# Mixer of a two-layer block: per-head rows in DRAM, loads four heads ahead, softmax rows scaled on GpSimd

## The chip, the cores and the metric

The kernel runs on one NeuronCore of a Trainium2 chip. The metric is device time in microseconds of one launch: 3129.61 us is the median of three runs (3122.44 to 3131.08) of the kernel before. The traces are of one profiled execution each. Engines are named as in the profile: PE (TensorE matmul), PEld (its weight load), DVE (VectorE), ACT (ScalarE), POOL (GpSimd), SP (SyncE, which issues nearly all DMAs here).

## The reference, cut to what matters

A first block (gated delta rule plus banded attention, up to about 730 us of the trace) is untouched. Its output enters a second block of two layers. Each layer is a feed-forward half, the mixer, a second feed-forward half and a per-layer embedding step. Only the mixer changes; x is [512, 1024], all in float32.

```python
def hybrid_mixer(h, ...):
    z = h @ w_in
    q_lat, kv_lat, k_rope, qkv_d = jnp.split(z, [c0, c1, c2], axis=-1)
    q = (rmsnorm(q_lat, q_norm) @ w_q_up).reshape(B, S, MLA_HEADS, MLA_NOPE + MLA_ROPE)   # 8 x (64 + 32)
    q_rope = apply_rope(q[..., MLA_NOPE:], cos_m, sin_m)
    kv = (rmsnorm(kv_lat, kv_norm) @ w_kv_up).reshape(B, S, MLA_HEADS, MLA_NOPE + MLA_V)
    k_rope = apply_rope(k_rope[:, :, None, :], cos_m, sin_m)[:, :, 0]                     # one, shared by 8 heads
    o_mla = mla_attention(q_nope, q_rope, k_nope, k_rope, v_mla)        # causal softmax, 512 x 512
    qd, kd, vd = [t.reshape(B, S, DIL_HEADS, DIL_HEAD_DIM) for t in jnp.split(qkv_d, 3, axis=-1)]   # 8 x 64
    o_dil = dilated_attention(apply_rope(qd), apply_rope(kd), vd)       # three strides, merged
    merged = jnp.concatenate([rmsnorm(o_mla, ...), rmsnorm(o_dil, ...)], axis=-1)
    return merged @ w_out
```

Each of the 16 heads is softmax(q k + mask) v over 512 tokens; "m" heads are the 8 latent heads (96 rows of q and k), "d" heads the 8 dilated ones (64 rows).

## The kernel before

Activations are feature-major tiles [128, 8, 512]. A float32 operand is kept as a high part and a low part (names ending in H and L), and a product is three matmul passes over them. A scheduler lays down the order of each engine ahead of the run, so the order on an engine is not the order of the code; a DMA on SP waits its turn in SP's row, and at most eight are under way.

The mixer (L1184 to L1425 of the function that the diff touches) goes through these stages, shown with the times of layer 0:

- The projections (1100 to 1197 us): q and k of the dilated heads come from the generator `dil`, called `fill`, in steps of 24 matmuls (psn<-xn). Four steps (g = 0, heads d0 to d3) run here; four steps (g = 1, heads d4 to d7) are filler for later. Every result is split into H and L in a tile `so` of three buffers and stored to DRAM by `out()` (L1207; the store is L1210).
- The latent stage (1197 to 1240 us): 60 matmuls on latH and latL make q and k of the latent heads and their v; `out()` stores QR, QN, KN; L1182 stores VM from a tile `vo` of two buffers. KR is the shared rope part of k.
- The attention loop (1240 to 1410 us). `scores(n)` loads q and k of head n into `qh` and `kh` (two buffers each) and v into `vh`: an m head takes five loads for q and k (L1336 to L1340), a d head eight loads of 32 rows (L1348, L1349). `head_scores` then does for four blocks of 128 queries, 128, 256, 384 and 512 keys wide: matmuls psg<-kh,qh on PE (psg has three buffers), mask and row maximum on DVE (L1145, to tile S, maximum in mn), exponential on ACT (L1147), and the reciprocal of the row sums on DVE (L1149, rd). `head_values` transposes S on PE (L1162, psx<-ident,S, ten matmuls), splits it into ptH and ptL (ACT, DVE), and multiplies by v (L1172, twelve matmuls); ACT copies the result to om or od (L1397).
- `normed` (L1357 to L1365) divides by the row sums after that: for each pair of heads eight matmuls (L1363, ident times rd spread over 64 columns) put 1/sum into psn, and DVE multiplies om or od by it (L1365).
- The heads go d0 to d3, m0 to m7, d4 to d7. The loop body of head n takes a step of filler (`fill`, `late`, and `first`, which is half of the output product) and calls `scores(n + 2)`.
- The tail (1405 to 1425 us): root-mean-square norms (`group`, L1309), the output product with weights wo, and the residual onto h, the [128, 8, 512] float32 tile (2 MB) of the residual stream, which sits in SBUF through the whole mixer.

Before the diff, a d head is loaded so:

```python
for y in range(2):
    for z in range(2):
        o = 64 * z + 32 * y
        nc.sync.dma_start(qf[o:o + 32, 0], QD[g, y, r, z])
        nc.sync.dma_start(kf[o:o + 32], KD[g, y, r])
```

## Time and profile before

| what | us |
|---|---|
| median of three runs | 3129.61 |
| the profiled execution, its own time | 3144.24 |
| its span, first to last instruction | 3142.3 |
| mixer of layer 0, of layer 1 | 1100 to 1425, 2310 to 2640 |
| attention stretch of layer 0, of layer 1 | 1240 to 1410, 2450 to 2617 |

The rows further down come from five views. The page gives busy time by engine and the chain of work that ended last. The list of waits says what ended an engine's idle time. The timeline lists instructions with their start and duration; a bracket gives the idle time before an instruction and what released it. The windows give busy time by engine for a stretch, with the granted TensorE clock (1.00 is 2.4 GHz, 0.50 is 1.2 GHz) and the traffic. The groups by line give count, busy time and mean duration.

### The profile page before, as it was taken

The page shows a single profiled execution, that of the slowest core. Times are in us where ns is not written, and L with a number is a line of the kernel's source. Part 1 is how long each engine was busy: PE and PEld are TensorE (multiplying, and loading weights), DVE is VectorE, ACT ScalarE, POOL GpSimd, SP SyncE. Part 2 cuts the span into 40 slices and gives each one's busy share as a digit, 9 for nine tenths or more (in the row PEclk, how much of TensorE's full clock was granted, in tenths as well). Part 3 has the DMA queues.
Part 4 walks back from the last instruction along what each step waited for, and adds up shares of the span by engine and source line. Part 5 has one row for each costly group of instructions (what it writes and reads, how often), then busy time and mean ns, then how long its engine had stood idle before and what let it go on. Part 6 is the DMA issues. An engine that isn't in the chain of part 4 may idle for free.

```text
span 3142.3 us, 41998 instructions
## 1 busy us (share of the span) xinstructions
PE 2853.6 (91%) x16048; PEld 2392.3 (76%) x16048; DVE 1747.3 (56%) x3733; ACT 1085.4 (35%) x2062; POOL 344.7 (11%) x199
## 2 busy tenths in 40 slices
PE   7999699999999997887999988999989787999987
PEld 2877588678888885667888878888887566888877
DVE  6678907666333475468523378423376457723357
ACT  3443225443222233563322234322233464322223
POOL 3023211422000011002000022000011001000010
PEclk8999769999999998998999998999999898999998
DMA  5325341443222136542222221322234643222321
GB/s 198 98 94 173 91 125 46 146 141 102 100 88 99 59 116 219 149 137 91 94 94 97 91 94 54 111 95 97 88 83 166 178 144 118 95 94 88 100 74 54
DMA packets 151584, 344.29 MB, mean 110 GB/s; under 512 B 37616, under 2 KB 58480, under 8 KB 150872
## 3 DMA queue, kind: packets, MB, share of 16 engines
q1 hardware_dynamic: 142168, 318.55, 31.9%
q10 hardware_dynamic: 9216, 23.07, 2.1%
q8 instruction: 126, 2.06, 0.3%
q14 instruction: 74, 0.61, 0.1%
HBM read 292.02 MB, written 49.54 MB: 109 GB/s over the span
## 4 chain that ended last, share of the span: by engine, by line
PE 71%; DVE 15%; ACT 4%; DMA 4%; issue 3%; POOL 2%; SPq 0%; ACTq 0%; DVEq 0%; POOLq 0%
PE psg L87 31%; PE psx L87 27%; PE psn L87 2%; PE psx L1172 2%; DVE ss L160 2%; DVE big L512 1%; ACT wH L78 1%; DMA wraw<-in_wo 1%; PE psn L141 1%; DVE wL L80 1%; ACT S L1147 1%; DMA wraw<-in_wvd 1%; DVE h L191 1%; DVE cy L386 1%; DVE xnL L105 1%
## 5 line engine op out<-in xcount | busy, mean ns | idle before, releaser
L78 ACT ACTIVATE wH<-wraw 128x1024 fp32r<-128x1024 f32 (+2 forms) x445 | 445.1, 1002 | 1149.7 <-PE psg L87 564.8
L80 DVE TENSOR_TENSOR wL<-wraw,wH 128x1024 fp32r<-128x1024 f32 (+3 forms) x353 | 406.4, 1153 | 458.9 <-ACT wH L78 458.2
L87 PE MATMUL psg<-xnH,wH 128*128 128x512 f32 (+3 forms) x1528 | 549.2, 361 | 11.8 <-ACT xnH L101 6.4
L87 PE MATMUL psg<-xnL,wH 128*128 128x512 f32 (+3 forms) x1528 | 548.9, 360 | 8.8 <-DVE xnL L105 8.8
L87 PE MATMUL psg<-xnH,wL 128*128 128x512 f32 (+3 forms) x1528 | 549.3, 360 | 4.4 <-POOL wL L80 4.4
L80 POOL TENSOR_TENSOR wL<-wraw,wH 128x1024 fp32r<-128x1024 f32 x92 | 224.9, 2451 | 2139.6 <-ACT wH L78 927.2
L87 PE MATMUL psx<-xnH,wL 128*128 128x512 f32 (+1 forms) x1120 | 391.2, 349 | 1.6 <-POOL wL L80 1.6
L87 PE MATMUL psx<-xnH,wH 128*128 128x512 f32 (+1 forms) x1120 | 392.1, 350 | 0.1
L87 PE MATMUL psx<-xnL,wH 128*128 128x512 f32 (+1 forms) x1120 | 392.0, 350 | 0.0
L87 PEld LDWEIGHTS psg<-xnH,wH 128*128 128x128 f32 (+2 forms) x1528 | 297.3, 195 | 52.8 <-ACT xnH L101 8.0
L87 PEld LDWEIGHTS psg<-xnL,wH 128*128 128x128 f32 (+2 forms) x1528 | 297.7, 195 | 49.9 <-DVE xnL L105 11.4
L87 PEld LDWEIGHTS psg<-xnH,wL 128*128 128x128 f32 (+2 forms) x1528 | 297.9, 195 | 45.3 <-POOL wL L80 5.3
L87 PEld LDWEIGHTS psx<-xnH,wL 128*128 128x128 f32 x1120 | 217.1, 194 | 28.4 <-POOL wL L80 1.9
L87 PEld LDWEIGHTS psx<-xnH,wH 128*128 128x128 f32 x1120 | 217.7, 194 | 26.9 <-ACT wH L78 0.3
L87 PEld LDWEIGHTS psx<-xnL,wH 128*128 128x128 f32 x1120 | 217.2, 194 | 25.8
L1056 DVE TENSOR_TENSOR fa<-fs,psx 128x512 f32<-128x512 f32 (+1 forms) x104 | 62.9, 605 | 270.0 <-PE psx L87 268.9
L87 PE MATMUL psg<-aH,wH 128*128 128x512 f32 (+1 forms) x464 | 159.2, 343 | 0.0
L87 PE MATMUL psx<-aL,wH 128*128 128x512 f32 (+1 forms) x464 | 158.8, 342 | 0.0
L87 PE MATMUL psg<-aL,wH 128*128 128x512 f32 (+1 forms) x464 | 158.5, 342 | 0.0
L87 PE MATMUL psx<-aH,wL 128*128 128x512 f32 (+1 forms) x464 | 158.4, 341 | 0.0
L87 PE MATMUL psx<-aH,wH 128*128 128x512 f32 (+1 forms) x464 | 158.4, 341 | 0.0
L87 PE MATMUL psg<-aH,wL 128*128 128x512 f32 (+1 forms) x464 | 158.3, 341 | 0.0
(568 smaller groups left out, 4756.1 us busy)
## 6 DMA issues: line engine op xcount, KB each, us to landing
wraw<-in_gu SPq DMA_DIRECT2D x176, 512.0 KB
wraw<-in_dn SPq DMA_DIRECT2D x64, 448.0 KB
wraw<-in_dn SPq DMA_DIRECT2D x32, 512.0 KB
wraw<-in_wmod SPq DMA_DIRECT2D x24, 512.0 KB
wraw<-in_wrest ACTq DMA_DIRECT2D x24, 512.0 KB
wraw<-in_wo SPq DMA_DIRECT2D x24, 512.0 KB
wraw<-in_win SPq DMA_DIRECT2D x22, 512.0 KB
kh<-KD SPq DMA_DIRECT2D x64, 128.0 KB
```

What stands on the lines that cost most here:

```text
L78: nc.scalar.activation(H[:, :n], raw[:, :n], AF.Copy)
L80: e.tensor_tensor(L[:, :n], raw[:, :n], H[:, :n].bitcast(F32), op=ALU.subtract)
L87: self.nc.tensor.matmul(ps, lhsT=l, rhs=r, start=start and i == 0, stop=stop and i == m - 1)
L105: e.tensor_tensor(L, src, H.bitcast(F32), op=ALU.subtract)
L141: self.nc.tensor.matmul(ps[:, 128 * c:128 * c + 128], lhsT=rs[:, c:c + 1].to_broadcast([128, 128]), rhs=self.ident, start=True, stop=True)
L160: nc.vector.tensor_tensor(self.a[i], self.a[i], q, op=ALU.add)
L191: nc.vector.tensor_tensor(hk, hk, t, op=ALU.add)
L386: nc.vector.scalar_tensor_tensor(y, cb[:, o + j:o + j + n], cw[:, j:j + 1], y, op0=ALU.mult, op1=ALU.add)
L512: nc.vector.tensor_tensor(tm, A[:112, i:i + 1, i + 1:].to_broadcast([112, n, n]), A[:112, i + 1:, i + 1:].rearrange("q j c -> q c j"), op= ...
L1056: nc.vector.tensor_tensor(a, s, pu[:, :n], op=ALU.mult)
L1147: nc.scalar.activation(S, S, AF.Exp, bias=mn[:, i:i + 1], scale=-1.0, accum_out=den[:, i:i + 1])
L1172: nc.tensor.matmul(pv[:, 128 * j:], lhsT=V[:, j, v:v + 64], rhs=R[b][:, o0:o0 + n], start=z == 0 and y == 0, stop=z == 3 and y == 2)
```

## The change

- DRAM layout: each head has its rows together, QM and KM [8, 96, 2, 512] for m heads, QD and KD [8, 64, 2, 512] for d heads. `out()` takes a list of destinations and makes two or four smaller stores of one tile where it made one. The shared rope part of k is stored into all eight heads by two stores of 32 x 8 x 512.
- `load()`: an m head takes two loads of 96 rows, a d head four of 64 rows. qh and kh have four buffers each, in a pool that takes the room of h. Four heads are loaded right after the fourth step of `fill`, ahead of the stores of the latent stage in the code, and then one head per loop step, for n + 6.
- h is stored to DRAM (hd) after the last read of it, and loaded again after the loop. For that its pool is opened after that of xn.
- The rows of S are multiplied by 1/sum on POOL, four instructions per head (L1153 of the changed kernel); `normed` is gone, with its matmuls and its DVE multiplication.
- The loop begins at n = -2 and calls scores(n + 2) first in its body; the step of filler comes after it, and the norm of the m half (`group(om, 0)`) stands at n = 12 where it stood at 13; `first` advances two steps from n = 13 where it advanced four from 14.

The core of the diff:

```diff
-            def out(src, dst, n=128):
+            def out(src, dsts, n=128):
                 t = pr.tile([128, 2, T], F32R, name="so", bufs=3)[:n]
                 self.split(t[:, 0], t[:, 1], src)
-                nc.sync.dma_start(dst, t.bitcast(F32))
+                m = n // len(dsts)
+                for i, d in enumerate(dsts):
+                    nc.sync.dma_start(d, t[m * i:m * i + m].bitcast(F32))
...
+            def load():
+                kind, h = seq[len(qks)]
+                k = pq.tile([128, 2, T], F32R, name="kh", bufs=4)
+                q = pq.tile([128, 2, T], F32R, name="qh", bufs=4)
+                if kind == "m":
+                    nc.sync.dma_start(qf[:96], QM[h])
+                    nc.sync.dma_start(kf[:96], KM[h])
+                else:
+                    for z in range(2):
+                        r = slice(64 * z, 64 * z + 64)
+                        nc.sync.dma_start(qf[r, 0], QD[h, :, z])
+                        nc.sync.dma_start(kf[r], KD[h])
...
                 self.less()
+                hd = self.dram(f"hd{l}", [128, 8, T])
+                nc.sync.dma_start(hd, self.h)
+                self.hctx.close()
...
                 for _ in range(4):
                     next(fill)
-                out(kr[0], KR, 32)
+                self.pq = self.pool(qctx, "qk", 1, "right")
+                for _ in range(4):
+                    load()
...
+        rd = p.tile([128, 4], F32, name="rd", bufs=3)
+        nc.vector.reciprocal(rd, den)
+        for i, S in enumerate(Ss):
+            nc.gpsimd.tensor_tensor(S, S, rd[:, i:i + 1].to_broadcast([128, S.shape[-1]]), op=ALU.mult)
...
-            cur = [scores(0), scores(1)]
+            cur = []
             late, first = self.ple_products(pr, l, "n"), early()
-            for n in range(16):
+            for n in range(-2, 16):
+                if n + 2 < 16:
+                    cur.append(scores(n + 2))
+                if n + 6 < 16:
+                    load()
...
-                if n < 14:
-                    cur.append(scores(n + 2))
...
-                if h % 2:
-                    normed(kind, h // 2)
...
+            qctx.close()
+            self.h = self.pool(self.hctx, "hrow", 1, "right").tile([128, 8, T], F32, name="h")
+            nc.sync.dma_start(self.h, hd)
```

Where the scheduler puts this, at three places of layer 0. First SP, from the stores of the last dilated k of g = 0 to the latent stores (QN, KN before; QM, KM after). Before:

```order
L1210 DMA KD_9672<-so 128x1024
L1210 DMA KR_9670<-so 32x1024
L1210 DMA QR_9669<-so 128x1024 x2
L1210 DMA QN_9667<-so 128x1024
L1210 DMA KN_9668<-so 128x1024
L1210 DMA QN_9667<-so 128x1024
L1210 DMA KN_9668<-so 128x1024
L1210 DMA QN_9667<-so 128x1024
L68 DMA wraw<-in_win 128x1024
```

After, beginning with the last two of the sixteen loads that follow the KD stores:

```order
L1268 DMA qh<-QD_9672 64x512
L1269 DMA kh<-KD_9673 64x1024
L1319 DMA KM_9671<-so 32x8x512 x2
L1216 DMA QM_9670<-so 8x16x1024 x2
L1216 DMA QM_9670<-so 64x1024 x2
L1216 DMA KM_9671<-so 64x1024 x2
```

The sixteen loads of heads d0 to d3 moved from behind the latent stores (single ones stood between the VM stores) to ahead of all of them, and the weights of the g = 1 filler, which were loaded between the QD, KD and QN stores, now stand between the second and the third pair of VM stores.

Second PE, where the scores of head d0 begin. Before:

```order
L87 MATMUL psn<-xnH,wL 128x512
L87 MATMUL psg<-kh,qh 128x128 x2
L87 MATMUL psg<-kh,qh 128x256 x2
L87 MATMUL psg<-kh,qh 128x384 x2
L87 MATMUL psg<-kh,qh 128x512 x2
L1162 MATMUL psx<-ident,S_10727 128x128
L1162 MATMUL psx<-ident,S_10733 128x128 x2
L1162 MATMUL psx<-ident,S_10739 128x128 x3
L1162 MATMUL psx<-ident,S_10745 128x128 x4
L1363 MATMUL psn<-ident,rd 64x128 x4
```

After:

```order
L87 MATMUL psg<-wH,latH 128x512
L87 MATMUL psg<-wH,latL 128x512
L87 MATMUL psg<-wL,latH 128x512
L87 MATMUL psg<-kh,qh 128x128 x2
L87 MATMUL psg<-kh,qh 128x256 x2
L87 MATMUL psg<-kh,qh 128x384 x2
L87 MATMUL psg<-kh,qh 128x512 x2
L87 MATMUL psg<-kh,qh 128x128 x2
L87 MATMUL psg<-kh,qh 128x256 x2
L87 MATMUL psn<-xnH,wH 128x512
L87 MATMUL psg<-kh,qh 128x384 x2
```

Before, filler stands ahead of the first scores (50 of the 96 matmuls of g = 1 do), and the transposes of a head follow directly on its own scores; after, the last latent matmul is followed by the scores of heads d0, d1 and d2, all 96 filler matmuls stand behind the first scores, and the first transposes follow after 24 of them.

Third PE in the latent heads of the loop. Before, with the transposes of the head whose scores stand just above them:

```order
L87 MATMUL psg<-kh,qh 128x128 x3
L87 MATMUL psg<-kh,qh 128x256 x3
L87 MATMUL psg<-kh,qh 128x384 x3
L87 MATMUL psg<-kh,qh 128x512 x3
L1162 MATMUL psx<-ident,S_11210 128x128
L1162 MATMUL psx<-ident,S_11217 128x128 x2
```

After: between the transposes of one head (L1166) and its products with v (L1176) stand scores of a later head and a step of `late`.

```order
L1166 MATMUL psx<-ident,S_10970 128x128
L87 MATMUL psg<-kh,qh 128x128 x3
L87 MATMUL psg<-kh,qh 128x256 x3
L87 MATMUL psg<-kh,qh 128x384 x3
L87 MATMUL psn<-wH 128x512
L1176 MATMUL psx<-ptH_11292,vh 64x512
```

The heads' own scores no longer stand directly ahead of their transposes anywhere in the loop.

## Rows read from the trace of the kernel before

**Rows 1.** The page: busy time by engine, traffic, and the chain by engine.
```profile
PE 2853.6 (91%) x16048; PEld 2392.3 (76%) x16048; DVE 1747.3 (56%) x3733; ACT 1085.4 (35%) x2062; POOL 344.7 (11%) x199
...
DMA packets 151584, 344.29 MB, mean 110 GB/s; under 512 B 37616, under 2 KB 58480, under 8 KB 150872
...
PE 71%; DVE 15%; ACT 4%; DMA 4%; issue 3%; POOL 2%; SPq 0%; ACTq 0%; DVEq 0%; POOLq 0%
```
**Rows 2.** Windows: us, busy by engine (instructions), clock, DMA share, GB/s.
```profile
1197.00:1226.00 29.00, 24.25 (x94) 17.83 (x92) 18.27 (x26) 11.00 (x19) 4.33 (x3) 0.94 0.77 282
1240.00:1410.00 170.00, 147.44 (x848) 109.81 (x848) 90.67 (x266) 95.54 (x243) 2.51 (x2) 0.92 0.52 154
...
1380.00:1390.00 10.00, 7.55 (x41) 4.65 (x40) 6.92 (x23) 6.81 (x22) 0.00 (x0) 1.00 0.03 13
...
1400.00:1410.00 10.00, 8.47 (x61) 6.97 (x59) 3.94 (x5) 5.50 (x10) 0.00 (x0) 0.90 0.73 242
```
**Rows 3.** Waits of PE, 1240 to 1410: total us, times, longest us.
```profile
PE psg L87 <- DMA kh<-KD: 14.0, 1, 14.0
PE psg L87 <- DVE mn L1145: 5.1, 5, 2.2
PE psx L1172 <- DVE ptL L105: 4.7, 5, 1.1
PE psx L1162 <- ACT S L1147: 4.7, 16, 1.1
```
**Rows 4.** The same list in layer 1, 2450 to 2617.
```profile
PE psg L87 <- DMA kh<-KD: 15.6, 1, 15.6
```
**Rows 5.** Timeline of PE at the first scores: start, us, instruction, [idle before <-releaser].
```profile
1225.26 0.39 PE L87 MATMUL psn<-xnL,wH 128*128 128x512 f32 x1
1225.49 0.40 PE L87 MATMUL psn<-xnH,wL 128*128 128x512 f32 x1
1239.86 2.69 PE L87 MATMUL psg<-kh,qh 128*128 128x128 f32 x8 [13.97 <-DMA kh<-KD]
...
1244.78 1.09 PE L1363 MATMUL psn<-ident,rd 128*64 128x128 f32 x8
```
**Rows 6.** Timeline of SP, issues of the latent stage.
```profile
1207.72 0.32 SPq L1210 DMA_DIRECT2D QN<-so  x1
...
1213.30 0.32 SPq L1210 DMA_DIRECT2D KN<-so  x1
...
1231.30 1.87 SPq L1182 DMA_DIRECT2D VM<-vo  x2
...
1234.74 1.77 SPq L1182 DMA_DIRECT2D VM<-vo  x2
...
1237.19 0.41 SPq L1349 DMA_DIRECT2D kh<-KD  x1
```
**Rows 7.** Timeline of ACT: a split that waits for a store.
```profile
1211.95 0.60 ACT L101 ACTIVATE so<-psg 128x512 fp32r<-128x512 f32 x1 [0.62 <-DMA QN<-so]
```
**Rows 8.** Groups by line on PE, 1240 to 1410: busy us, mean ns, idle before.
```profile
L1363 PE MATMUL psn<-ident,rd 128*64 128x128 f32 x128 | 18.0, 304 | 1.4 <-DVE rp_u L1117 1.4
```
**Rows 9.** Groups by line on DVE, 1240 to 1410.
```profile
L80 DVE TENSOR_TENSOR wL<-wraw,wH 128x512 fp32r<-128x512 f32 (+1 forms) x13 | 11.6, 896 | 9.6 <-ACT wH L78 9.3
```
**Rows 10.** Timeline of POOL in the first block: scaling by a broadcast column.
```profile
510.29 4.46 POOL L998 TENSOR_TENSOR wS<-wS,wrd 128x512 f32<-128x512 f32 x4
```
**Rows 11.** Groups of tile so, all of the span: duration ns min/median/max.
```profile
L105 DVE TENSOR_TENSOR so<-rp_u,so x26: 670/692/2219, 139.1 to 2484.2; 128x512 fp32r<-128x512 f32 x24, 64x512 fp32r<-64x512 f32 x2
...
L105 DVE TENSOR_TENSOR so<-psg,so x16: 680/683/693, 1207.0 to 2431.3; 128x512 fp32r<-128x512 f32 x16
```
**Rows 12.** The chain that ended last, at the end of the attention.
```profile
1404.94 1.06 ACT wH L78
1406.02 1.23 DVE wL L80
...
1415.93 4.28 DMA wraw<-in_wo
```

More of the change, by code (lines that the diff above doesn't have):

```diff
@@ L1225, in dil @@
                         for y in range(2):
-                            out(o[y], (QD, KD)[z][g, y])
+                            out(o[y], [(QD, KD)[z][4 * g + i, 32 * y:32 * y + 32] for i in range(4)])
                         yield
@@ L1278, in mixer @@
                     next(fill)
-                out(kr[0], KR, 32)
+                self.pq = self.pool(qctx, "qk", 1, "right")
+                for _ in range(4):
+                    load()
+                t = pr.tile([128, 2, T], F32R, name="so", bufs=3)[:32]
+                self.split(t[:, 0], t[:, 1], kr[0])
+                for z in range(2):
+                    nc.sync.dma_start(KM[:, 64:96, z].rearrange("h p t -> p h t"),
+                                      t[:, None, z].bitcast(F32).to_broadcast([32, 8, T]))
                 Q, KV = (latH[:, 0:2], latL[:, 0:2]), (latH[:, 2:3], latL[:, 2:3])
@@ L1290, in mixer @@
                 for z in range(2):
-                    out(o[z], QR[z])
+                    out(o[z], [QM[:, 64 + 16 * z:80 + 16 * z]])
                 Wq = self.w(I["wqn"][l], 8, 128)
@@ L1296, in mixer @@
                     self.acc(ps, self.fm([w_[:, 2 * z:2 * z + 2] for w_ in Wq], Q, range(2), 0, F))
-                    out(ps, QN[z])
+                    out(ps, [QM[2 * z + i, :64] for i in range(2)])
                     ps = self.ps()
                     self.acc(ps, self.fm([w_[:, z:z + 1] for w_ in Wk], KV, range(1), 0, F))
-                    out(ps, KN[z])
+                    out(ps, [KM[2 * z + i, :64] for i in range(2)])
                 Wv = self.w(I["wkv"][l], 1, 512)
@@ L1357, in normed @@
-            def normed(kind, x):
-                rd, o = rds[kind, x], (om if kind == "m" else od)[:, x]
-                ps = self.ps("n")
-                for y in range(2):
-                    for i in range(4):
-                        nc.tensor.matmul(ps[64 * y:64 * y + 64, 128 * i:128 * i + 128], rhs=self.ident,
-                                         lhsT=rd[:, y, i:i + 1].to_broadcast([128, 64]), start=True, stop=True)
-                nc.vector.tensor_tensor(o, o, ps, op=ALU.mult)
+                nc.sync.dma_start(v.bitcast(F32), (VM if kind == "m" else VD)[h])
@@ L1384, in mixer @@
                     next(fill, None)
-                elif n < 12:
+                elif n >= 13:
+                    for _ in range(2):
+                        next(first, None)
+                elif n > 4:
                     next(late, None)
-                if n == 13:
+                if n == 12:
                     group(om, 0)
-                if n < 14:
-                    cur.append(scores(n + 2))
-                if n >= 14:
-                    for _ in range(4):
-                        next(first, None)
                 pv = self.ps("x")[:64]
@@ L1403, in mixer @@
             actx.close()
+            qctx.close()
+            self.hctx = ExitStack()
+            self.h = self.pool(self.hctx, "hrow", 1, "right").tile([128, 8, T], F32, name="h")
+            nc.sync.dma_start(self.h, hd)
             self.more()
```

57 lines of the change are left out of this document (21 added, 36 removed).

## The prediction

> **What bounds the kernel now.** I read the page first. PE is busy 91% of the span and carries 71% of the chain that ended last [rows 1], so a change pays where it takes work off PE or where PE is idle. The second view is the table of windows over the mixer of layer 0: the attention stretch lasts 170.00 us and PE works 147.44 us of it, while DVE works 90.67, ACT 95.54 and POOL 2.51 [rows 2]. PE is the bound there, with 22.56 us of idle time. The third view, the list of waits, names that idle time and one larger piece ahead of it: 14.0 us on the load of kh, once [rows 3], 15.6 us in layer 1 [rows 4]. The timeline shows the place: filler ends at about 1225.9, and the first scores start at 1239.86 [rows 5]. The fourth view, SP's timeline, says why: the loads of the first head stand between the stores of VM, and the last load of kh is issued at 1237.19, behind the VM store of 1234.74 [rows 6].
>
> Inside the stretch the waits are mn 5.1, ptL 4.7 and S 4.7 us and smaller ones [rows 3]. The order shows their cause: PE has no other head's scores between a head's scores and its transposes, so the row maximum, exponential and split of one head lie open.
>
> All sums are against the profiled execution, 3144.24 us; the median of the runs shown is 3129.61, so a difference is scaled by 0.9953. About 0.3%, 9.4 us, is what a measurement of this kernel can tell from no change. Both layers have the same code and the same idle time within 2 us, so I work out one layer and double it.
>
> **The change part by part.**
>
> *First scores: -5 us.* The loads of heads d0 to d3 now precede the latent stores on SP. They are released when the last KD store has landed; I put that at about 1202, one store link ahead of the QN store of 1207.72 [rows 6] (an estimate). They are 3 MB with 16 issues. At 282 GB/s, the rate of this stretch [rows 2], they take about 11 us, but the latent stores go behind them. These stores are paced by `so`: its three buffers are refilled only when a store has landed, and ACT waits on a QN store issued at 1207.72 until 1211.95 [rows 6, 7], 4.2 us; a link from one store to the one that takes its buffer is 1207.72 to 1213.30, 5.6 us [rows 6]. The shared k rows (1 MB where 128 KB were stored) and the halves of QM and KM add no links, only issues. With the last load issued at about 1210, the first KM store landed at 1215, three links end at 1232, and the last latent matmuls and the v copies put head 0's scores at about 1235, against 1239.86. Bounds: the loads cost nothing (1231, -9), or stores wait until all 3 MB have landed and one more link is needed (1246, +6).
>
> *Filler that used the wait: +11.5 us.* Before, 50 of the 96 filler matmuls of g = 1 ran ahead of the first scores, in time that PE would otherwise have waited for stores; after, none does. They are spaced 0.23 us apart [rows 5]: 50 x 0.23 = 11.5 us that now lie in the stretch. This is certain from the order, so it has one end only.
>
> *A thin stretch behind the first scores: +5 us.* The weights of that filler are now queued behind the second pair of VM stores. Two pairs are 1234.74 - 1231.30 = 3.44 us apart [rows 6]; a weight load took 4.28 us and its split 1.06 + 1.23 [rows 12]; 3.44 + 4.28 + 2.29 = 10.0. Until then PE has the scores of two heads, 2 x 2.69 = 5.4 us [rows 5]. The rest, 4.6, is idle, and I round it up to 5 for the third head. It is 0 if the first VM pair is stored well ahead of the scores, 8 if the weights also wait for the third pair.
>
> *`normed` off PE: -17 us.* 128 matmuls are busy 18.0 us in the stretch and 1.4 us more are waited for [rows 8]; part of the 18.0 is overlap of neighbours, since eight of them span 1.09 us [rows 5] with the last one's tail over the next matmul: 16 x 1.06 = 17. They stand on the engine that bounds the stretch. The 0.69 us of DVE per pair goes too, and counts only at the end, where the norm waits for it (-1).
>
> *The scaling on POOL: 0 of its own.* The same form (a tile times a broadcast column) took 4.46 us for 4 x 512 columns at the least favourable, 2.2 ns a column [rows 10]. A head has 1280 columns: 2.8 us, 45 us for 16 heads, on an engine with 2.51 us of work in 170. It adds 2.8 us between exponential and transpose of a head. What hides it is one or two heads' scores, products and filler, some 9 us of PE per head. At the last head no scores are left, and half of it, 1.4, may show; it is in the extras.
>
> *Contention of POOL with DVE.* The split so<-rp_u, which runs beside POOL, took up to 2219 ns where its median is 692; the same split from psg never exceeded 693 [rows 11]. So DVE instructions that read only SBUF can be stretched by 1.5 us beside POOL. In the stretch these are the 13 wL splits [rows 9] and about 16 of the norms. DVE is 79 us short of the stretch's length, so I take 1 of the extras' 4 us for it, bound 0 to 4. The Trainium skill, "SBUF — State Buffer", section "SBUF: two separate sides", says the same and more sharply: a DVE instruction with two SBUF inputs and a GpSimd instruction that reads SBUF hold a shared port in turn, for a whole instruction. By that rule the 13 splits could each wait one scaling, and the sum would be some 4 us a layer later; by the row's median, nothing.
>
> *Waits in the stretch: -12 us.* With the scores of two later heads ahead, S (4.7), the wait of `normed` (1.4) and most of mn (5.1) have other work in front; of ptL (4.7) and ptH half remains, since scores stand there only for some heads. I take 12 of the 22.56 us. Bounds: 2 (only S shrinks, and turns into a wait for POOL) and 18 (all but the tail).
>
> *Clock: -1.5 us.* Behind the long wait the granted clock is low: 0.92 in the stretch [rows 2]. A shorter wait gives some of it back, but the thin stretch takes part. Bounds -5 and 0.
>
> *h, and other extras: +4 us.* The store of h (2 MB) runs in the projections, with no reader behind it until its room is reused by the loads. The reload waits for the last scores, and in SP's row it stands ahead of ten loads of wo. DMA is idle at 1380 to 1390 (0.03 of the engines) [rows 2], but wo is on the chain at 1415.93 [rows 12]. At the 242 GB/s of 1400 to 1410 [rows 2] 2.1 MB take 8.7 us; if it lands in the idle stretch it costs nothing, if it delays wo all of it. I take 2 to 3, and with POOL's two terms 4; bounds 0 and 9.
>
> Sum per layer: -5 + 11.5 + 5 - 17 - 1 - 12 - 1.5 + 4 = -16. Both layers: -32. 3144.24 - 32 = 3112.2, times 0.9953 is 3098 on the scale of the median.
>
> **The rivals.**
>
> *Attention runs dense.* The thin stretch vanishes (0 for +5), waits fall by 18 and the reload is hidden (+1): -5 + 11.5 - 17 - 1 - 18 - 1.5 + 1 = -30 per layer, -60, 3070. For it: no engine but PE has more than 96 us of work in 170. Against it: psg has three buffers, and each is freed by DVE one after the other.
>
> *Given back.* The first scores stay at 1240 (0), and the waits only shrink by 6, because POOL's scaling and the split of S take the places of S and mn: 11.5 + 5 - 17 - 1 - 6 + 5 = -2.5 per layer, -5, about 3125. For it: PE's idle time in the latent stage rises by the filler that left it, and the same `so` links still set its length.
>
> *Slower by SP's row.* Sixteen loads stand ahead of every store that frees `so`. If they move at the page's mean rate, 110 GB/s [rows 1], instead of 282, 3 MB take 28 us, the stores begin at about 1230 and the first scores at 1254 or later, +15 and more: 15 + 11.5 + 5 - 17 - 1 - 8 - 1 + 4 = +8.5 per layer, +17, 3147. It decides from first scores at about 1251 on when the other terms are those of the forecast (the sum without the first term is -11), and from 1245 when the waits shrink by 6 alone. For it: short rows (2 KB and 4 KB a partition) and eight under way at most. Against it: the latent stage already moves 282 GB/s.
>
> That the change doesn't do what it says is excluded by the order: scores of three heads stand ahead of the first transposes, and no `normed` is left.
>
> The stores of the q rope part are now 8 x 16 rows. The Trainium skill, "DMA: Bandwidth & Descriptors", section "Why a DMA increments its semaphore by 16 and not by 1", states that the number of engines is the largest divisor up to 16 of the slowest dimension, 8 here where 128 rows have 16. No run here shows it. By it those two stores would take twice as long, and as links of `so` add some 2 us to the first scores.
>
> **How the numbers follow.** Forecast 0.60, dense 0.18, given back 0.13, slower 0.09. The forecast's own range is 3082 to 3114, from waits of 5 to 16 and first scores from 1231 to 1243. The range for 8 in 10 is 3070 to 3125: it reaches to the dense case and the case that gives back, and leaves out the slower one, half of what lies above 3125 and what lies below 3070. Faster by over 0.3% (under 3120.2): dense, nearly all of the forecast and little of given back, 0.79. Within 0.3%: most of given back, 0.12. Slower by over 0.3%: 0.09.
>
> **What would show it.** First scores at about 1235 (layer 0), with the wait on kh gone or replaced by one on stores of `so` or VM; a gap in the filler 5 us behind them; no matmuls of ident times rd; POOL with some 45 us in the stretch, and no long wait of the transposes on POOL; PE with 142 us of work in a stretch of about 157. Wrong: first scores past 1250, a wait of PE on S released by POOL in every head, or wo waiting behind the load of h.

## The result, and the profile after

The changed kernel takes 3099.14 us (median of six runs, 3096.79 to 3111.47) against 3130.35 for the kernel before on the same chips (six runs). The ratio is 0.9898, with a 95% interval of 0.9874 to 0.9922. The forecast was 3098, so the total is right. The working behind it is right only in part: several terms had the wrong size, one the wrong sign, and that their errors cancelled is luck.

The page of the changed kernel, with the lines that answer [rows 1]:

```profile
span 3096.4 us, 41739 instructions
...
PE 2790.7 (90%) x15792; PEld 2360.1 (76%) x15792; DVE 1738.7 (56%) x3717; ACT 1079.6 (35%) x2062; POOL 434.7 (14%) x327
...
PE 70%; DVE 17%; issue 4%; ACT 3%; DMA 3%; POOL 2%; SPq 1%; DVEq 0%; ACTq 0%; POOLq 0%
```

PE lost 62.9 us of work and POOL gained 90. The spans differ by 45.9 us, more than the medians (31.2). Part of that is not the change's: the first block, which the change doesn't touch, ran at a lower clock in the profiled execution of before. The windows of 384 to 404 us, of before and then of after (us, busy by engine, clock, DMA share, GB/s):

```profile
384.00:404.00 20.00, 20.00 (x174) 16.06 (x173) 12.33 (x9) 5.53 (x10) 2.36 (x1) 0.50 0.37 103
```

```profile
384.00:404.00 20.00, 20.00 (x233) 16.05 (x231) 13.24 (x9) 9.13 (x16) 3.85 (x2) 1.00 0.40 109
```

The granted clock was 0.50 (1.2 GHz) in one and 1.00 (2.4 GHz) in the other, PE was busy all the time in both, and it did 174 and 233 matmuls. The feed-forward half ahead of the mixer begins at 732.1 us in before and at 720.4 in after: 11.7 us that are not the change's. Over all the profiled executions of this study that point lies between 709.9 and 734.7, so differences of a few us are read from the mixers themselves: from the last instruction of tile fs in the half ahead of a mixer to the first in the half behind it. On ACT's timeline, before:

```profile
1057.97 0.58 ACT L1055 ACTIVATE fs<-psg 128x512 f32<-128x512 f32 x1
...
1487.06 0.38 ACT L1055 ACTIVATE fs<-psg 128x256 f32<-128x256 f32 x1
...
2265.21 0.58 ACT L1055 ACTIVATE fs<-psg 128x512 f32<-128x512 f32 x1
...
2689.43 0.38 ACT L1055 ACTIVATE fs<-psg 128x256 f32<-128x256 f32 x1
```

And after:

```profile
1046.31 0.58 ACT L1056 ACTIVATE fs<-psg 128x512 f32<-128x512 f32 x1
...
1457.62 0.38 ACT L1056 ACTIVATE fs<-psg 128x256 f32<-128x256 f32 x1 [0.44 <-PE psg L87]
...
2232.87 0.58 ACT L1056 ACTIVATE fs<-psg 128x512 f32<-128x512 f32 x1
...
2644.59 0.38 ACT L1056 ACTIVATE fs<-psg 128x256 f32<-128x256 f32 x1
```

The mixers took 429.1 and 424.2 us, and take 411.3 and 411.7: -17.8 and -12.5, together -30.3 where -32 was forecast. The stretch between them gives 2.9 more, the one behind the second 1.1.

| part of a mixer, layer 0 / layer 1 | before | after | change | forecast |
|---|---|---|---|---|
| end of the feed-forward half to the first scores | 181.9 / 184.9 | 189.8 / 188.6 | +7.9 / +3.7 | -5 |
| first scores to the next feed-forward half | 247.2 / 239.3 | 221.5 / 223.1 | -25.7 / -16.2 | -11 |

**Why the first scores come later.** SP's timeline after, from the last KD stores to the first latent ones (of the sixteen loads the first and the last; beside [rows 6]):

```profile
1188.55 3.58 SPq L1216 DMA_DIRECT2D KD<-so  x8
1192.17 0.50 SPq L1268 DMA_DIRECT2D qh<-QD  x1
...
1202.19 0.45 SPq L1269 DMA_DIRECT2D kh<-KD  x1
1202.94 1.38 SPq L1319 DMA_DIRECT2D KM<-so  x2
1204.67 9.88 SPq L1216 DMA_DIRECT2D QM<-so  x4
```

The first three splits of latent results on ACT (beside [rows 7]), the first scores on PE (beside [rows 5]), and the window ahead of the first split:

```profile
1211.51 0.60 ACT L101 ACTIVATE so<-psg 128x512 fp32r<-128x512 f32 x1 [16.58 <-DMA KM<-so]
1214.49 0.60 ACT L101 ACTIVATE so<-psg 128x512 fp32r<-128x512 f32 x1 [2.38 <-DMA QM<-so]
1217.01 0.60 ACT L101 ACTIVATE so<-psg 128x512 fp32r<-128x512 f32 x1 [1.92 <-DMA QM<-so]
```

```profile
1236.14 0.66 PE L87 MATMUL psg<-kh,qh 128*128 128x128 f32 x2 [6.17 <-issue]
```

```profile
1196.00:1211.00 15.00, 0.00 (x0) 0.00 (x0) 0.00 (x0) 0.00 (x0) 0.00 (x0) 0.53 1.01 251
```

For 15 us no engine does anything; the DMA engines move the loads of d0 to d3 and the 1 MB of shared k rows at 251 GB/s (1.01 of their time), and the store that frees `so` lands behind them.

To set this beside the forecast, 11.7 us have to be added to the times of after, since the half ahead of the mixer began that much earlier. The loads then begin at 1203.8, where 1202 was forecast, so the stage began when it should. The first store frees its buffer at 1223.2, where 1215 was forecast: 8 us late. The last latent split ends at 1238.6, where 1232 was: the links between took 1.5 us less than forecast. The first scores come at 1247.8, where 1235 was, so another 6 us are lost behind the last split. There the text allowed 3 us for the copies of v; but `vo` has two buffers, and its third copy waits for a VM store that stands behind the stores of all latent results in SP's row:

```profile
1234.33 0.38 ACT L1184 ACTIVATE vo<-psg 128x256 fp32r<-128x256 f32 x1 [7.35 <-DMA VM<-vo]
```

```profile
1235.62 0.42 DVE L1185 TENSOR_TENSOR vo<-psg,vo 128x256 fp32r<-128x256 f32 x1 [0.45 <-ACT vo L1184]
```

The last copy ends at 1236.04 and the first scores start at 1236.14. The profile names no releaser for PE's 6.17 us there; that the scores wait for the buffer of psg which these copies empty is read from the times, and a run below with a longer wait at the same place names vo.

**Why the attention is shorter than forecast.** Groups by line on PE from the first scores to the last norm of the loop (1239.8 to 1412.3 before, 1236 to 1385.7 after; count, busy us, mean ns, idle before). Before:

```profile
L1172 PE MATMUL psx<-ptH,vh 128*64 128x512 f32 (+3 forms) x128 | 33.5, 340 | 5.5 <-DVE ptL L105 4.0 <-ACT ptH L101 1.4
L87 PE MATMUL psg<-kh,qh 96*128 96x128 f32 (+7 forms) x160 | 32.7, 347 | 19.1 <-DMA kh<-KD 14.0 <-DVE mn L1145 5.1
L1162 PE MATMUL psx<-ident,S 128*128 128x128 f32 x160 | 31.7, 316 | 4.9 <-ACT S L1147 4.7
```

After:

```profile
L87 PE MATMUL psg<-kh,qh 96*128 96x128 f32 (+7 forms) x160 | 36.3, 352 | 8.5 <-issue 6.2 <-DVE mn L1146 2.4
L1176 PE MATMUL psx<-ptH,vh 128*64 128x512 f32 (+3 forms) x128 | 31.9, 327 | 10.8 <-DVE ptL L105 7.3 <-ACT xnH L101 3.2
L1166 PE MATMUL psx<-ident,S 128*128 128x128 f32 x160 | 20.9, 275 | 0.1
```

The same 160 transposes were busy 31.7 us and are busy 20.9. Their wait for S went from 4.7 to nothing, as forecast, but 10.8 us more had been hidden in what the profile counts as busy: before, a transpose started when its block of S was ready and the next one had to wait, after, ten run on end. The waits of the products with v grew instead of shrinking, from 5.5 us to 10.8 (ptL 4.0 to 7.3). In all, PE was idle 21.5 us of these 149.7, hardly less than the 22.56 of 170.00 before [rows 2].

### The profile page after: what moved, and what is told of

Same layout as the page of the kernel before. It is cut to its first block, busy times and chain, and to the rows that moved or that the text cites. A ratio compares the mean times of both kernels' runs of the same rounds, so it can differ in the third digit from the quotient of the medians.

```text
span 3096.4 us, 41739 instructions
## 1 busy us (share of the span) xinstructions
PE 2790.7 (90%) x15792; PEld 2360.1 (76%) x15792; DVE 1738.7 (56%) x3717; ACT 1079.6 (35%) x2062; POOL 434.7 (14%) x327
## 4 chain that ended last, share of the span: by engine, by line
PE 70%; DVE 17%; issue 4%; ACT 3%; DMA 3%; POOL 2%; SPq 1%; DVEq 0%; ACTq 0%; POOLq 0%
PE psg L87 31%; PE psx L87 27%; PE psn L87 3%; DVE ss L160 2%; PE psx L1176 2%; DVE h L191 1%; DVE big L512 1%; PE psn L141 1%; DVE xnL L105 1%; DMA QM<-so 1%; DVE wL L80 1%; DVE rq_y L120 1%; PE psn L133 1%; DVE cy L386 1%; DVE ptL L105 1%
## 5 line engine op out<-in xcount | busy, mean ns | idle before, releaser
L87 PEld LDWEIGHTS psx<-xnL,wH 128*128 128x128 f32 x1120 | 214.3, 191 | 25.7
L1057 DVE TENSOR_TENSOR fa<-fs,psx 128x512 f32<-128x512 f32 (+1 forms) x104 | 62.9, 605 | 269.5 <-PE psx L87 268.3
```

The costliest lines, as they stand in the source:

```text
L87: self.nc.tensor.matmul(ps, lhsT=l, rhs=r, start=start and i == 0, stop=stop and i == m - 1)
L1057: nc.vector.tensor_tensor(a, s, pu[:, :n], op=ALU.mult)
```

## The experiments

All verdicts go by the ratio to runs of before on the same chip, and by the two mixers' lengths (411.3 and 411.7 in the changed kernel, 823.0 together, 853.3 before). Every version but one is faster than before beyond its interval, and all of these intervals overlap the changed kernel's own (0.9874 to 0.9922). Each kernel has one trace. So a difference of a few us between the mixers of two versions is a hint, and the time doesn't confirm it.

**The scaling on GpSimd undone.**

```diff
-        for i, S in enumerate(Ss):
-            nc.gpsimd.tensor_tensor(S, S, rd[:, i:i + 1].to_broadcast([128, S.shape[-1]]), op=ALU.mult)
...
+                if h % 2:
+                    normed(kind, h // 2)
```

> The changed kernel with one part undone: the rows of S are not scaled on GpSimd; the 128 small matmuls of ident and rd per layer and the multiplication of om and od on DVE are back. Theory (PE bounds the attention stretch and these matmuls lie on it): 17 us per layer come back less a few, 3126 to 3133. Rival (the gain came from the look-ahead, and PE has idle time that takes the small matmuls in): 3105 to 3112.

It took 3097.44 us, ratio 0.9893 (0.9867 to 0.9919), mixers 411.0 and 413.1: no difference. The theory (17 us a layer lie on the path) fails, and the time lies below even the rival's 3105 to 3112. From first scores to the last norm, this kernel and then the changed one:

```profile
1226.30:1376.00 149.70, 138.12 (x872) 113.31 (x872) 99.64 (x283) 100.36 (x256) 5.03 (x4) 0.96 0.66 197
```

```profile
1236.00:1385.70 149.70, 128.19 (x744) 104.51 (x744) 97.11 (x276) 101.73 (x256) 51.53 (x68) 0.92 0.66 197
```

Both stretches last 149.7 us. With 128 matmuls more PE is busy 9.9 us more and idle 9.9 us less (11.6 against 21.5); the granted clock is 0.96 against 0.92. PE's waits for ptL in this mixer are 3.5 us here and 8.8 in the changed kernel. So once scores run ahead, PE is no longer alone in setting the end: taking work off it lengthens its waits for DVE and ACT.

**The scaling on GpSimd alone, in the kernel before.**

```diff
         nc.vector.reciprocal(dens, den)
+        for i, S in enumerate(Ss):
+            nc.gpsimd.tensor_tensor(S, S, dens[:, i:i + 1].to_broadcast([128, S.shape[-1]]), op=ALU.mult)
...
-                if h % 2:
-                    normed(kind, h // 2)
```

> The kernel before with one part of the change alone: the rows of S scaled on GpSimd, no small matmuls, no multiplication of om and od. Layout, loads, buffers and loop order as before. Theory (17 us of PE per layer go, and most of it is kept although scaling now stands between exponential and transposes): 3096 to 3108 against 3130. Rival (without look-ahead the scaling, 2.8 us a head and 45 us a layer, lies open in every head): at or above 3130, with PE waiting for S from POOL in every head.

It took 3236.45 us, ratio 1.0347 (1.0322 to 1.0371), mixers 482.1 and 475.2: the rival, and larger. PE's longest wait in the attention of layer 0, one such place on its timeline, and the scaling that it waits for on POOL's:

```profile
PE psx L1164 <- POOL S L1151: 38.4, 30, 3.6
```

```profile
1297.33 0.48 PE L1164 MATMUL psx<-ident,S 128*128 128x128 f32 x1 [3.65 <-POOL S L1151]
```

```profile
1296.87 3.73 POOL L1151 TENSOR_TENSOR S<-S,rd 128x128 f32<-128x128 f32 x4 [11.55 <-DVE rd L1149]
```

Without scores of other heads in front, the four scalings of a head (3.73 us) lie between its exponential and its transposes, and the filler that could stand there has been used up earlier: all 96 matmuls of g = 1 ran ahead of the first scores, where the trace of before has 48 there. The granted clock fell too. From the first scores to the last products it is 0.68, where it was 0.92 [rows 2]:

```profile
1228.00:1450.00 222.00, 160.60 (x672) 115.05 (x672) 89.87 (x256) 97.91 (x248) 47.61 (x65) 0.68 0.40 118
```

PE is idle 61.4 of these 222.0 us, and busy 160.60 us with fewer matmuls than before (147.44 us for 848 [rows 2]). So the part that costs nothing in the changed kernel costs 51 to 53 us a layer by itself, through waits, a lower clock and the order that the scheduler gave it; their shares are not separated.

**The order in the loop body undone.**

```diff
-                if n + 2 < 16:
+                if n < 0:
                     cur.append(scores(n + 2))
-                if n + 6 < 16:
                     load()
-                if n < 0:
                     continue
...
                 if n == 12:
                     group(om, 0)
+                if n + 2 < 16:
+                    cur.append(scores(n + 2))
+                if n + 6 < 16:
+                    load()
```

> The changed kernel with the order inside the loop body as before: step of filler, norm of the m half, then scores(n + 2) and the load for n + 6. Theory (the scores of later heads put ahead of a head's transposes are what fills the waits inside a head): the waits of PE on ptL, S and mn grow by 5 to 10 us per layer, 3109 to 3119. Rival (scores are two heads ahead in either order and the scheduler moves them on its own): within 5 us of 3099.

3094.42 us, ratio 0.9897 (0.9872 to 0.9923), mixers 409.8 and 409.8: the rival. The order in which the loop body is written doesn't matter here.

**Both undone, so that layout, early loads, four buffers and the trip of h stand alone** (the two diffs above together).

> The changed kernel with two parts undone at once, the scaling on GpSimd (back to small matmuls) and the order inside the loop body; layout, early loads, four buffers and the trip of h stay. Theory (the loads carry the whole gain): 3092 to 3100, as with either part undone alone. Rival (the two parts stand in for each other, and one of them is needed): 3110 to 3125.

3105.53 us, ratio 0.9924 (0.9893 to 0.9955), mixers 414.6 and 416.5. It lies between theory and rival: 22 of the 30 us in the mixers are there without the two parts. The other 4 us a layer may need one of them; the times don't settle it.

**The four early loads moved behind the stores of the latent q and k.**

```diff
-                self.pq = self.pool(qctx, "qk", 1, "right")
-                for _ in range(4):
-                    load()
                 t = pr.tile([128, 2, T], F32R, name="so", bufs=3)[:32]
...
+                self.pq = self.pool(qctx, "qk", 1, "right")
+                for _ in range(4):
+                    load()
                 Wv = self.w(I["wkv"][l], 1, 512)
```

> The changed kernel with one thing moved: the four load() calls stand behind the stores of the latent q and k (ahead of the v products) instead of ahead of all latent stores. Theory (in the changed kernel 3 MB of loads stand ahead of the stores that free `so`; ACT waits 16.58 us for the KM store and all engines stand still from 1196 to 1211): the split of the first latent result starts some 14 us earlier, the loads then cost some 5 of it, first scores 8 to 12 us earlier per layer, the kernel near 3079 us against 3099. Rival (the DMA engines move the same bytes in either order, so first scores wait for the loads instead): a wait on kh of 10 us or more comes back, time within 8 us of 3099.

3109.58 us, ratio 0.9928 (0.9905 to 0.9951), mixers 414.8 and 415.2: 3.5 us a layer worse, where the theory wanted 10 better. The first split does come earlier, with a wait of 4.44 us, but the first scores then wait for vo:

```profile
1213.87 0.60 ACT L101 ACTIVATE so<-psg 128x512 fp32r<-128x512 f32 x1 [4.44 <-DMA KM<-so]
```

```profile
1254.04 0.66 PE L87 MATMUL psg<-kh,qh 128*128 128x128 f32 x2 [19.47 <-DVE vo L1185]
```

The loads now stand ahead of the VM stores, which free `vo`, and PE's row has the v products ahead of the scores. In both kernels the ring of buffers that is stored behind the 3 MB stands still: so in the changed one (16.58 us), vo here (19.47 us on PE).

**One early load, three behind the v products.**

```diff
-                for _ in range(4):
-                    load()
+                load()
...
                         self.v_out(pr, ps[:, 256 * y:256 * y + 256], VM[4 * y:4 * y + 4, :, b, :], 4)
+                for _ in range(3):
+                    load()
```

> The changed kernel with the load of head d0 alone ahead of the latent stores, and those of d1 to d3 behind the v products in the code. Theory (loads in SP's row ahead of the stores that free so and vo hold the latent stage up, 16.58 us ahead of its first split): that wait shrinks to about 4 us, first scores come 8 to 12 us earlier per layer, 3077 to 3085. Rival (the stage is bound by the bytes it moves, at DMA shares near 1, so what leaves its head comes back at its tail as a wait for d1 to d3 and for the weights of the filler): 3095 to 3108.

3107.03 us, ratio 0.9934 (0.99 to 0.9968), mixers 414.7 and 418.1. Both are right in part: the wait ahead of the first split is 8.17 us (4 were expected), the first scores come 7.9 and 5.8 us earlier (181.9 and 182.8), and more than that is lost behind them. PE waits for the next head, and the weights of the filler come behind the late loads, so that its steps run in a bunch:

```profile
1200.15 0.60 ACT L101 ACTIVATE so<-psg 128x512 fp32r<-128x512 f32 x1 [8.17 <-DMA KM<-so]
```

```profile
PE psg L87 <- DMA kh<-KD: 5.7, 1, 5.7
```

**Two buffers and two early loads.**

```diff
-                k = pq.tile([128, 2, T], F32R, name="kh", bufs=4)
-                q = pq.tile([128, 2, T], F32R, name="qh", bufs=4)
+                k = pq.tile([128, 2, T], F32R, name="kh", bufs=2)
+                q = pq.tile([128, 2, T], F32R, name="qh", bufs=2)
...
-                for _ in range(4):
+                for _ in range(2):
                     load()
...
-                if n + 6 < 16:
+                if n + 4 < 16:
```

> The changed kernel with one size changed: qh and kh have two buffers where they had four, and loads run two heads ahead (two heads early, then n + 4). Theory (four buffers are what lets scores run ahead of transposes): waits of PE for kh come back in the loop, 3112 to 3125. Rival (rows together and early loads are enough, two buffers feed the loop): 3095 to 3102; since 1.5 MB less stands ahead of the latent stores it can even be 6 us a layer faster, 3088.

3090.79 us, ratio 0.9864 (0.9788 to 0.994), mixers 407.7 and 407.2: the rival, to its faster end. The wait ahead of the first latent split is 9.87 us in place of 16.58:

```profile
1215.72 0.60 ACT L101 ACTIVATE so<-psg 128x512 fp32r<-128x512 f32 x1 [9.87 <-DMA KM<-so]
```

So the wait grows with what stands in front of the store: 4.44 us with the loads behind the latent q and k, 8.17 with one head ahead, 9.87 with two, 16.58 with four. No wait for kh comes back in the loop. Four buffers are not needed, and by the mixers the two heads more that they load early cost 4 us a layer.

**The shared k rows in a tensor of their own.**

```diff
-                for z in range(2):
-                    nc.sync.dma_start(KM[:, 64:96, z].rearrange("h p t -> p h t"),
-                                      t[:, None, z].bitcast(F32).to_broadcast([32, 8, T]))
+                nc.sync.dma_start(KR, t.bitcast(F32))
...
-                    nc.sync.dma_start(kf[:96], KM[h])
+                    nc.sync.dma_start(kf[:64], KM[h, :64])
+                    nc.sync.dma_start(kf[64:96], KR)
```

> The changed kernel with the shared k rows in a tensor of their own again: one store of 128 KB in place of two of 512 KB, and a third load for each m head. Theory (the 16.58 us ahead of the first latent split are the wait for 3 MB of loads in front): the wait shortens by the 0.9 MB less, some 3.5 us at 245 GB/s, 3092 to 3097. Rival (it is the store into eight heads that is slow): the wait falls below 5 us, 3075 to 3085. Third: the m heads' extra load costs as much as this gives, 3097 to 3102.

3114.26 us, ratio 0.994 (0.9909 to 0.9972), mixers 418.4 and 421.7. None of the three was right. The wait ahead of the first latent split is 14.76 us in place of 16.58, so it is in the main the loads that are waited for; the first scores come 2.4 us earlier in layer 0 (187.4) and 0.8 in layer 1, but behind them 10 us are lost. The scheduler's order had changed there, with steps of `late` in bunches. Whether the third load itself costs anything can't be told from this run.

**The layout alone, in the kernel before.** In `scores(n)`, with `out()` and its stores as in the change:

```diff
-                    nc.sync.dma_start(qf[0:64], QN[h // 2, r])
-                    for z in range(2):
-                        nc.sync.dma_start(qf[64 + 16 * z:80 + 16 * z], QR[z, 16 * h:16 * h + 16])
-                    nc.sync.dma_start(kf[0:64], KN[h // 2, r])
-                    nc.sync.dma_start(kf[64:96], KR)
+                    nc.sync.dma_start(qf[:96], QM[h])
+                    nc.sync.dma_start(kf[:96], KM[h])
```

> The kernel before with one part of the change alone: each head's rows together in DRAM, so two loads of 96 rows or four of 64 rows; loads inside scores(n) as before, two buffers, h stays in SBUF, small matmuls on PE. Measure beside the time: the distance in the trace from the last instruction of tile fs (feed-forward half ahead of the mixer) to the first of the next half, 429 and 424 us before, 411 and 412 in the changed kernel. Theory (what pays is that loads start apart from scores and ahead of the latent stage, which lets scores run ahead of transposes): the layout alone gives 0 to 5 us a layer, 3120 to 3130. Rival (fewer and longer loads are the gain): mixers at 412 to 416, time 3098 to 3106.

3105.13 us, ratio 0.9917 (0.9889 to 0.9945), mixers 417.3 and 411.7: 24.3 of the 30.3 us. The rival is the nearer by its time, but not for its reason alone. The wait for kh at the first scores is still there (10.1 us, 14.0 before), and the scheduler's order on PE has changed with the layout: no filler of g = 1 stands ahead of the first scores (48 matmuls in the trace of before), and in many heads other work stands between the scores and the transposes. This run can't tell shorter loading from that order. PE's transposes, in 1226.2 to 1390:

```profile
L1162 PE MATMUL psx<-ident,S 128*128 128x128 f32 x160 | 23.7, 286 | 0.6 <-ACT S L1147 0.6
```

**The layout undone, all else as in the changed kernel** (QN, QR, KN, KR, QD, KD and the five and eight loads of before, in `load()`).

```diff
-                    nc.sync.dma_start(qf[:96], QM[h])
-                    nc.sync.dma_start(kf[:96], KM[h])
+                    nc.sync.dma_start(qf[0:64], QN[h // 2, r])
+                    for z in range(2):
+                        nc.sync.dma_start(qf[64 + 16 * z:80 + 16 * z], QR[z, 16 * h:16 * h + 16])
+                    nc.sync.dma_start(kf[0:64], KN[h // 2, r])
+                    nc.sync.dma_start(kf[64:96], KR)
```

> The changed kernel with one part undone: the layout in DRAM and its loads (five for q and k of an m head, eight of 32 rows for a d head) and single stores are those of before; early loads, four buffers, scaling on GpSimd and loop order stay. Theory (early loads carry the gain whatever their layout): mixers at 408 to 414 us, 3092 to 3102. Rival (the rows together are needed: SP issues 32 loads of some 0.5 us ahead of the latent stores in place of 16, and eight loads per head in the loop): 8 us ahead of the first latent split and some more in the loop, mixers at 420 or more, 3114 or more.

3093.17 us, ratio 0.9892 (0.9855 to 0.993), mixers 408.2 and 408.5: the theory. The layout is not needed when the loads come early; by the mixers the kernel is 3 us a layer better without it. The first scores come 13 us earlier (176.4 and 175.7), although 32 loads stand ahead of most of the latent stores. Three things differ there. The loads of q begin 12.5 us earlier, because the scheduler put them between the QD and the KD stores (133.3 us behind the feed-forward half, 145.9 in the changed kernel). The shared k rows are one store of 128 KB. And the q rope part is stored in 128 rows, not in 8 x 16. On ACT's timeline the splits follow each other like this:

```profile
1218.68 0.60 ACT L101 ACTIVATE so<-psg 128x512 fp32r<-128x512 f32 x1 [9.22 <-DMA KR<-so]
1219.92 0.60 ACT L101 ACTIVATE so<-psg 128x512 fp32r<-128x512 f32 x1 [0.64 <-DMA QR<-so]
1221.16 0.60 ACT L101 ACTIVATE so<-psg 128x512 fp32r<-128x512 f32 x1 [0.64 <-DMA QR<-so]
```

The second and third split wait for the two stores of the q rope part (QR here, QM in the changed kernel), one store per tile in both. Here they follow after 1.24 us each; in the changed kernel the second comes 2.98 us after the first and the third 2.52 us later. The windows of the first of these links, in the changed kernel and then here:

```profile
1211.50:1214.50 3.00, 1.61 (x3) 0.83 (x3) 0.69 (x1) 0.61 (x2) 0.00 (x0) 0.50 0.53 198
```

```profile
1218.70:1219.90 1.20, 0.00 (x0) 0.00 (x0) 0.59 (x1) 0.58 (x1) 0.00 (x0) 0.50 1.02 406
```

While ACT waits for the store of 8 x 16 rows the DMA engines are busy for 0.53 of their time, at 198 GB/s; with stores of 128 rows they are busy throughout, at 406. No run separates the three differences. What this version gains ahead of the first scores it loses in part behind them: 231.8 and 232.8 us from first scores to the next half, against 221.5 and 223.1.

**Filler inside the latent stage,** on top of two buffers and two early loads, and the same with one early load and one behind the v products:

```diff
                     out(ps, [KM[2 * z + i, :64] for i in range(2)])
+                    if z == 1:
+                        next(fill)
```

> Two buffers and two early heads, and one step of filler more (24 matmuls) called inside the latent stage, after its second pair of products, to be done while PE waits for so. Theory (PE stands idle there for 12 to 19 us, and the filler left that place): 24 x 0.23 = 5.5 us a layer less than with two buffers alone, whose mixers took 408 and 407: 402, 3080. Rival (the weights of that step are 0.5 MB more ahead of the first scores, in a stage bound by bytes): 408, 3091.

> As the version with two buffers and one filler step inside the latent stage, but only head d0 is loaded ahead of the latent stores and d1 behind the v products. Theory (what stands in SP's row ahead of the latent stores delays them): 3 us a layer less than with two heads early, mixers at 399, 3074. Rival (d1 then comes late, as d1 to d3 did when one head alone was early, and PE waits on kh some 5 us): 405 or more.

With two heads early: 3103.77 us, ratio 0.9931 (0.9909 to 0.9953), mixers 413.0 and 413.0, worse than two buffers alone by 5 us a layer and than both figures expected. PE now waits 11.6 us ahead of a latent product for a split of weights (wkv), because their load moved behind the early loads and the latent stores in SP's row: it is issued at 1220.54, with two buffers alone at 1180.39. With one head early: 3088.52 us, ratio 0.9875 (0.9837 to 0.9912), mixers 407.7 and 405.2, the shortest pair of all, 812.9; but that is the rival's figure and not the 399 of the theory, and its wait for that split is 11.9 us as well.

Four versions are thus ahead of the changed kernel by their mixers: this last one with 812.9, two buffers with 814.9, the old layout with 816.7 and the old loop order with 819.6, against 823.0. Their intervals overlap with its own, so that they beat it in time is not shown.

## Why the prediction was right, and which of its steps were not

- **First scores, -5: wrong in sign.** They came 7.9 and 3.7 us later. The step that failed is that 3 MB of loads were given 11 us, but only their issue time was charged to the stores behind them. What is queued behind the loads in SP's row landed behind their bytes: with four heads in front the first split comes 165.2 us behind the feed-forward half, with none 153.3 (the loads moved), 11.9 us apart. A second step was left out: the VM stores wait in the same row, and the copies of v took 9 us where 3 were put. The bound (+6) held in layer 1 and not in layer 0.
- **The stores of 8 x 16 rows, some 2 us beside the sum: shown.** Their two links took 5.5 us where two of 128 rows took 2.5, with the DMA engines half busy in the first.
- **Filler, +11.5: right in kind.** Nothing of g = 1 ran ahead of the first scores. It wasn't measured by itself.
- **The thin stretch, +5: the size about right, the cause not.** In 1236 to 1256, PE worked 17.37 of 20 us at a clock of 0.70. Of the 2.6 us idle, 2.4 are waits of scores for the row maximum (mn); none is a wait for the weights of the filler, so the gap that was forecast there did not come.
- **`normed`, -17: wrong.** Undone, it changes the mixers by -0.3 and +1.4 us. The 18.0 us of [rows 8] are gone, and PE's waits and its lower clock took their place. The term was argued from PE as the bound of the stretch before, and the other half of the change ended that.
- **Waits, -12: right with the norm on PE, not without it.** In the kernel with the norm on PE, PE is idle 11.6 us, 11 less than the 22.56 before [rows 2]; in the changed kernel it is idle 21.5. S went to 0 and mn from 5.1 to 2.4 [rows 3], and ptL grew.
- **The transposes: a term that the sum didn't have.** They were busy 10.8 us less, and the list of idle time doesn't show that. In the sum it takes the place of most of what `normed` didn't give. PE worked 128.2 of 149.7 us, where 142 of 157 were forecast.
- **POOL, 0 of its own: right with the condition that it named.** The scalings took 46.5 us a layer (45 forecast), and no wait of PE on them is in the list. Without the cover they cost 51 to 53 us a layer, where the text put their cover at 9 us of PE per head.

```profile
L1153 POOL TENSOR_TENSOR S<-S,rd 128x128 f32<-128x128 f32 (+1 forms) x64 | 46.5, 757 | 109.5 <-DVE rd L1151 78.5 <-PE psx L1166 23.6 <-PE psg L87 4.9
```

- **POOL against DVE, 1 us, bound 4: within the bound.** The splits of weights on DVE, in the kernel with the norm on PE and then in the changed one:

```profile
L80 DVE TENSOR_TENSOR wL<-wraw,wH 128x1024 fp32r<-128x1024 f32 (+1 forms) x18 | 17.7, 983 | 5.1 <-ACT wH L78 5.0
```

```profile
L80 DVE TENSOR_TENSOR wL<-wraw,wH 128x1024 fp32r<-128x1024 f32 (+1 forms) x18 | 18.6, 1033 | 9.2 <-ACT wH L78 9.2
```

  That is 0.9 us over 18 splits, and nine additions of squares took 4.7 us where they took 3.7. The mean hides that only three of these splits and two of the additions ran beside a scaling at all. Here one split and one addition did, and a split of the same size that ran alone:

```profile
1344.03 3.20 POOL L1153 TENSOR_TENSOR S<-S,rd 128x128 f32<-128x128 f32 x4 [2.42 <-PE psn L87]
```

```profile
1344.98 1.35 DVE L80 TENSOR_TENSOR wL<-wraw,wH 128x512 fp32r<-128x512 f32 x1 [1.09 <-ACT wH L78]
1346.26 1.25 DVE L160 TENSOR_TENSOR ss<-ss,ss_q 128x256 f32<-128x256 f32 x1
...
1367.39 0.68 DVE L80 TENSOR_TENSOR wL<-wraw,wH 128x512 fp32r<-128x512 f32 x1
```

  The split took 0.67 us longer and the addition 0.83 (0.42 alone), where a scaling lasts 0.757 us on average. The rule of the Trainium skill ("SBUF — State Buffer", section "SBUF: two separate sides") is that a DVE instruction with two SBUF inputs can wait a whole instruction of GpSimd. The trace agrees with it in this place; the sum stayed small because the two seldom met. The prediction's 4 us for that rule is also less than its own terms give: 13 splits times a scaling of 0.7 us are 9 us.
- **h and the wo weights, +3: too much.** The load of h was issued at 1349.24, with the DMA engines 0.43 busy from 1349 to 1375, and no wait for wo is on the chain behind 1375, where before had one of 4.28 us [rows 12].
- **Clock, -1.5: nothing.** 0.92 in the stretch before and after.

Summed: the first scores were mis-sized by +13 and +9 a layer, the rest by -15 and -5, and the total came out within 2 us of -32. The median was 1 us off. That is luck: no argument of the prediction ties the two errors together.

What carries the gain is settled in part. It is neither the scaling on GpSimd, nor the loop order, nor four buffers: without any one of them the gain stays. Either the rows together in DRAM or the loads apart from `scores` is enough for most of it, and with either of them the scheduler puts other work between a head's scores and its transposes, the transposes run on end (20.9 and 23.7 us busy, 31.7 before) and the wait for S is gone. That this order is the cause is likely and not shown. What stays open is the share of the scheduler's order: small edits moved the mixers by 3 to 10 us through steps of filler that fell elsewhere (the shared k rows, the filler in the latent stage), and no run holds the order fixed.

## What to carry to other kernels

Before an operation is taken off the busiest engine, ask what paces that engine once the rest of the change is in: here 14 us of matmuls less gave nothing, and the same step without its cover cost 50 us a layer. A load issued early is paid by the stores behind it in the same row (4 to 17 us of wait here, by the heads in front), so load early what the first consumers need and no more. When two traces are set side by side, first take out what differs ahead of the stretch, 11.7 us here. Where a chain of short instructions is fed one at a time, its busy time holds waits that no list of idle time shows; compare it with the same instructions run on end.

## What the runs showed of the hardware that was not expected

The 128x128 transposes count as 316 ns each, 31.7 us in all, when they are fed block by block, and as 275 ns and 20.9 us when ten run on end. In the first block, whose code both kernels share, two executions with PE busy throughout a stretch of 20 us were granted 0.50 and 1.00 of the clock. In both, the stretch of 370 to 380 us ahead of it had nearly the full clock (0.98 and 0.96) with PE busy throughout. And a store of 128 rows that is laid out as 8 x 16 kept the DMA engines busy for only half of their time: its links of the `so` ring took 2.98 and 2.52 us, where plain rows took 1.24.
